# Encoder block on one core: window pooling moved from vector adds to banded matmuls, with the order of TensorE's work in that stage written out

## The chip, the cores and the metric

The kernel is one program on one core of a Trainium2 chip. Its time is the device time of one execution in microseconds (us); the number compared is the median over several executions. The engines are TensorE (PE, matmuls, with PEld for its weight loads), VectorE (DVE), ScalarE (ACT), GpSimd (POOL) and SyncE (SP), whose queue issues nearly all transfers.

## The reference, cut to what matters

An encoder block on 512 tokens of 1024 channels: a normalised input `h`, one wide projection of it, a pooling mixer and an eight-head differential attention side by side, then a mixture of 16 experts. The pooling mixer is what the change is about:

```python
h = rms_norm(x, g_mix[l])
z = jnp.einsum('bsd,dc->bsc', h, w_in[l])
u_pool = z[..., :c_q]                       # 1024 channels, 4 groups of 256
...
for g, w in enumerate((2, 4, 8, 16)):       # one window width for each group
    lo = jnp.clip(t - w // 2, 0, S)
    hi = jnp.clip(t + w // 2, 0, S)
    win = jnp.take(csg, hi, axis=1) - jnp.take(csg, lo, axis=1)
    cnt = (hi - lo).astype(jnp.float32)[None, :, None]
    pooled = (win / cnt).astype(u.dtype) - ug[:, :, g]
    outs.append(jnp.einsum('bsc,cd->bsd', pooled, w_mix[g]))
```

For each channel, the mean over a window of tokens, less the token itself, goes through a 256x256 matrix of its group.

## The kernel before

Operands of the early matmuls are kept as a high and a low part (`split`: ACT writes the rounded high part, then DVE or POOL the remainder), and each product is three matmuls (`mm3`: high-high, high-low, low-high). The stages in order are: the pooling stage; the projections for the first attention head (`scq`: q and k, then `task("v", 0)`); eight attention heads, with the other projections filled in between; the output projection; the router; 16 experts, whose weights are streamed into a ring of slots.

Weights of the early stages come through a queue of their own: `add_w` lists them, `load_next` issues the transfer on SP into one of four `wraw` buffers and splits it into one of three `whl` tiles, and `weights()` hands out the next tile and loads up to two ahead. A `whl` tile is refilled when the matmuls that read it are done. `CFG` says for each kind whether DVE (V) or POOL (G) makes the low part.

In the pooling stage the projection of a group (48 matmuls of 512 columns, the weights stationary and the 512 tokens moving) lands in the two PSUM banks of an `sc` tile, with channels on partitions and tokens along the free axis. `windows(g, sc)` then works on VectorE: it scales by the tokens' norm `rbc`, adds shifted copies in doubling steps until the window is full (one step for width 2, four for width 16), corrects 8 columns at either border, divides and subtracts, and splits the result into `pooled`. `mix(g)` multiplies that with the group's matrix (12 matmuls) into `ip` banks, and `mo` gets the split result. `ip` has two banks, `at` two, `sc` two pairs.

The order of instructions on each engine comes from a planner, which runs the program through a cost model. Its order on TensorE puts the matmuls of neighbouring steps between one another. Only the last expert has an order written out by hand (`tc.manual_schedule`).

Of the kernel before, what the change touches and what calls it, by code (L numbers as in the profile page):

```python
# [41 lines left out]
CFG = {'wu': 'GVGG',  # L42
# [20 lines left out]
 'fills': (1, 0.3, 2, 0.5, 2.5, 1.5, 2, 1, 0.5),  # L63
 'tabs': 1}
# [28 lines left out]
def block_kernel(tc, a, out):  # L93
# [105 lines left out]
    for g in GROUPS:  # L199
        for j in range(2):  # L200
            add_w(a["w_c"][2 * g + j], eng=ENG[CFG["wu"][GROUPS.index(g)]])
            if g != 3 and j == 1:
                add_w(a["w_pool_mix"][g + 1], 512, cfg("wmix"))
    add_w(a["w_c"][8], eng=cfg("wq0"))
    add_w(a["w_c"][16], eng=cfg("wk0"))
# [14 lines left out]
    for h in range(NH):  # L220
        for kind, i in plan(h):
            if kind == "q":
                add_w(a["w_c"][8 + i], eng=cfg("wq"))
            elif kind == "k":
                add_w(a["w_c"][16 + i], eng=cfg("wk"))
            elif kind == "v":
                add_w(a["w_v"][i, 0], eng=cfg("wv"))
                add_w(a["w_v"][i, 1], eng=cfg("wv"))
            elif kind == "pool":
                add_w(a["w_c"][24 + i], eng=cfg("wg"))  # L230
                add_w(a["w_pool_out"][i], eng=cfg("wp"))
            else:
                add_w(a["w_c"][32 + i], eng=cfg("wga"))
    for d in range(KT):
        add_w(a["w_attn_out"][d], eng=cfg("wao"))
        if d < 3:
            add_w(a["w_c"][37 + d], eng=cfg("wga"))
# [9 lines left out]
    with pool("st", side="right") as st:  # L247
        first = []
# [16 lines left out]
        def load_x(k):  # L265
            xk = st.tile([P, S], F32, name="xk", bufs=5)
# [4 lines left out]
        part_w(0, 0, P)  # L271
        load_x(0)
        part_w(0, P, S)
        part_w(1, 0, S)
        load_x(1)
        load_x(2)
        part_w(0, S, D)
        load_x(3)
        part_w(1, S, D)
        for k in range(4, KT):  # L280
            load_x(k)
        SP.dma_start(cv, a["consts"])
        load_next()
        sc0 = psA.tile([P, 2, S], F32, name="sc")
        for k in range(KT):
            for j in range(2):
                w = loaded[j]
                mm3(sc0[:, j], w[:, 0, cols(k)], w[:, 1, cols(k)], hT[:, 0, k], hT[:, 1, k], k == 0, k == KT - 1)
# [12 lines left out]
        pr = bank("at")  # L301
        for t in range(NTT):
            T.transpose(pr[:, cols(t)], rn[:, t:t + 1].to_broadcast([P, P]), ident)
        A.copy(rbc, pr)
# [3 lines left out]
        bd = pl.tile([P, 4, 2, PAD], F32, name="bd")  # L308
        SP.dma_start(bd, a["border"])
        SP.dma_start(psc, a["pool_scale"])  # L310
        V.tensor_scalar(psc, psc, 0.5, None, op0=ALU.mult)
        pooled = {}

        def windows(g, sc):
            w = WINDOWS[g]
            pooled[g] = pl.tile([P, 2, 2, S], F32R, name="pooled", bufs=2)
            n = S + 2 * PAD
            for j in range(2):
                u = pl.tile([P, n], F32, name="u", bufs=2)
                V.memset(u[:, 0:PAD], 0.0)  # L320
                V.memset(u[:, S + PAD:], 0.0)
                V.tensor_tensor(u[:, PAD:S + PAD], sc[:, j], rbc, op=ALU.mult)
                cur, lo, hi, d = u, 0, n, 0
                while (1 << d) < w:
                    nx = pl.tile([P, n], F32, name="sw", bufs=2)
                    if d == 0:
                        V.tensor_tensor(nx[:, 1:n], cur[:, 0:n - 1], cur[:, 1:n], op=ALU.add)
                        lo = 1
                    else:
                        q = 1 << (d - 1)  # L330
                        V.tensor_tensor(nx[:, lo + q:hi - q], cur[:, lo:hi - 2 * q], cur[:, lo + 2 * q:hi],
                                        op=ALU.add)
                        lo, hi = lo + q, hi - q
                    cur = nx
                    d += 1
                for b, o in ((0, PAD), (1, S)):
                    V.tensor_tensor(cur[:, o:o + PAD], cur[:, o:o + PAD], bd[:, g, b], op=ALU.mult)
                pq = pl.tile([P, S], F32, name="pq", bufs=2)
                V.scalar_tensor_tensor(pq, cur[:, PAD:S + PAD], 1.0 / w, u[:, PAD:S + PAD],
                                       op0=ALU.mult, op1=ALU.subtract)  # L340
                split(pooled[g][:, 0, j], pooled[g][:, 1, j], pq)
# [11 lines left out]
        def tables():  # L353
# [11 lines left out]
            pi, ang, nt, sh, ch = (st.tile([P, S], F32, name="xk", bufs=5) for _ in range(5))  # L365
# [19 lines left out]
        windows(3, sc0)  # L385
        for g in GROUPS[1:]:
            sc = psA.tile([P, 2, S], F32, name="sc")
            for j in range(2):
                run(hmul(sc[:, j], weights()))
            windows(g, sc)  # L390
            mix(g + 1)
            if g == CFG["tabs"]:
                tables()
        MASK = list(range(8, 16)) + list(range(8)) + list(range(16, 32))
        at_cm = pool("at", side="right")
        scq = psA.tile([P, 2, S], F32, name="sc")
        run(hmul(scq[:, 0], weights()))
        run(hmul(scq[:, 1], weights()))
        mix(0)
# [591 lines left out]
def _shape_constants():  # L991
# [11 lines left out]
    border = np.ones((4, 2, PAD), np.float32)  # L1003
    for g, w in enumerate(WINDOWS):
        cnt = np.clip(t + w // 2, 0, S) - np.clip(t - w // 2, 0, S)
        r = np.float32(w) / cnt.astype(np.float32)
# [89 lines left out]
```

## Time and profile before

| what | value |
|---|---|
| median of 3 runs | 1809.09 us (1806.86 to 1811.04) |
| the profiled execution | 1810.21 us, of which its span is 1808.4 us |
| TensorE busy (matmuls) | 1694.5 us, 94% of the span |
| VectorE, ScalarE, GpSimd busy | 570.6 us (32%), 339.3 us (19%), 220.0 us (12%) |
| bytes moved | 607.00 MB |
| mean granted TensorE clock | 0.973 |

Busy times are sums over the whole span, which has stages with different limits; a matmul's modelled duration overlaps the next one's, so the number of matmuls in a stretch says more than the busy time. The granted clock has no row before 11.8 us; the windows print 1.00 there.

### The profile page before, as it was taken

The page shows a single profiled execution, that of the slowest core. Times are in us where ns is not written, and L with a number is a line of the kernel's source. Part 1 is how long each engine was busy: PE and PEld are TensorE (multiplying, and loading weights), DVE is VectorE, ACT ScalarE, POOL GpSimd, SP SyncE. Part 2 cuts the span into 40 slices and gives each one's busy share as a digit, 9 for nine tenths or more (in the row PEclk, how much of TensorE's full clock was granted, in tenths as well). Part 3 has the DMA queues.
Part 4 walks back from the last instruction along what each step waited for, and adds up shares of the span by engine and source line. Part 5 has one row for each costly group of instructions (what it writes and reads, how often), then busy time and mean ns, then how long its engine had stood idle before and what let it go on. Part 6 is the DMA issues. An engine that isn't in the chain of part 4 may idle for free.

```text
span 1808.4 us, 20272 instructions
## 1 busy us (share of the span) xinstructions
PE 1694.5 (94%) x8296; PEld 863.2 (48%) x8296; DVE 570.6 (32%) x1330; ACT 339.3 (19%) x668; POOL 220.0 (12%) x193
## 2 busy tenths in 40 slices
PE   7999999999999999999999999998898989888898
PEld 5777887877873333333333333333333323233344
DVE  6865566663342212021220211122021212202023
ACT  4454555663221000000000000000000000000002
POOL 2453344444410000000000000000000000000000
PEclk9999999999999898998989999899999999999999
DMA  6332322222599999999999999999999999999997
GB/s 202 97 102 82 94 82 77 76 71 88 200 430 418 389 422 430 429 429 430 430 429 428 430 429 430 429 429 429 429 429 430 429 429 429 430 429 430 426 425 298
DMA packets 58973, 607.00 MB, mean 336 GB/s; under 512 B 8056, under 2 KB 8832, under 8 KB 32768
## 3 DMA queue, kind: packets, MB, share of 16 engines
q1 hardware_dynamic: 56320, 601.51, 80.0%
q0 software_dynamic: 2560, 4.20, 1.1%
q8 instruction: 65, 1.06, 0.2%
q14 instruction: 28, 0.23, 0.0%
HBM read 599.38 MB, written 2.10 MB: 333 GB/s over the span
## 4 chain that ended last, share of the span: by engine, by line
PE 53%; DMA 16%; DVE 7%; ACT 1%; issue 1%; POOL 0%; POOLq 0%; ACTq 0%; DVEq 0%
PE gu L786 23%; DMA sl<-in_w_down_dram 14%; PE mx L838 10%; PE mx L847 6%; PE mx L750 3%; DVE cmp L643 3%; DMA sl<-in_w_end_dram 2%; PE ip L124 1%; PE ip L125 1%; PE ip L123 1%; PE gu L885 1%; DVE cmp L646 1%; DVE ax L849 1%; PE gu L787 1%; PE gu L125 1%
## 5 line engine op out<-in xcount | busy, mean ns | idle before, releaser
L786 PE MATMUL gu<-sl,xs 128*64 128x512 f32 (+3 forms) x1556 | 626.7, 558 | 4.9 <-DMA sl<-in_w_up_dram 3.1
L787 PE MATMUL gu<-sl,xs 128*64 128x512 f32 (+3 forms) x1556 | 626.7, 558 | 0.0
L786 PEld LDWEIGHTS gu<-sl,xs 128*64 128x64 f32 x1556 | 209.4, 139 | 394.2 <-issue 377.4
L838 PE MATMUL mx<-sl,ax 128*64 128x512 f32 (+1 forms) x720 | 290.7, 559 | 34.7 <-DMA sl<-in_w_down_dram 29.0
L839 PE MATMUL mx<-sl,ax 128*64 128x512 f32 (+1 forms) x720 | 290.7, 559 | 0.0
L787 PEld LDWEIGHTS gu<-sl,xs 128*64 128x64 f32 x1556 | 209.4, 139 | 0.0
L838 PEld LDWEIGHTS mx<-sl,ax 128*64 128x64 f32 x720 | 95.8, 137 | 215.5 <-issue 158.7
L849 DVE TENSOR_TENSOR ax<-ax,mx 128x512 f32<-128x512 f32 x112 | 73.7, 685 | 384.9 <-PE mx L847 384.9
L118 POOL TENSOR_TENSOR whl<-wraw,whl 128x512 fp32r<-128x512 f32 x122 | 165.6, 1366 | 223.4 <-ACT whl L116 220.0
L960 POOL TENSOR_TENSOR fs<-fs,cv 128x1 f32<-128x1 f32 x4 | 2.6, 660 | 1269.0 <-DVE fs L959 1268.9
L792 DVE TENSOR_TENSOR act<-act,gu 128x512 f32<-128x512 f32 (+3 forms) x49 | 30.6, 629 | 393.3 <-PE gu L787 393.2
L847 PE MATMUL mx<-y,vv 64*128 64x512 f32 x240 | 118.6, 816 | 25.5 <-DVE ax L849 14.3
L116 ACT ACTIVATE whl<-wraw 128x512 fp32r<-128x512 f32 (+1 forms) x149 | 92.6, 625 | 102.1 <-PE ip L124 38.9
L643 DVE TENSOR_SCALAR_CACHE_REDUCE cmp<-mx,aff 128x384 f32<-128x384 f32 (+3 forms) x105 | 54.7, 521 | 148.9 <-PE mx L730 146.2
L123 PE MATMUL ip<-hT,whl 128*128 128x512 f32 x240 | 97.8, 407 | 0.0
L839 PEld LDWEIGHTS mx<-sl,ax 128*64 128x64 f32 x720 | 95.8, 137 | 0.0
L125 PE MATMUL ip<-hT,whl 128*128 128x512 f32 x240 | 94.5, 394 | 0.0
L124 PE MATMUL ip<-hT,whl 128*128 128x512 f32 x240 | 94.4, 393 | 0.0
L752 ACT COPY y<-mx 128x512 f32<-128x512 f32 x16 | 9.4, 585 | 452.8 <-PE mx L750 452.8
L847 PEld LDWEIGHTS mx<-y,vv 64*128 64x128 f32 x240 | 38.5, 222 | 100.4 <-DVE ax L849 76.1
L800 ACT COPY ax<-mx 128x512 f32<-128x512 f32 (+2 forms) x47 | 24.1, 549 | 310.6 <-PE mx L799 310.6
L750 PE MATMUL mx<-x,gm 128*64 128x512 f32 x256 | 58.4, 596 | 16.4 <-DVE gm L745 16.3
(246 smaller groups left out, 2007.6 us busy)
## 6 DMA issues: line engine op xcount, KB each, us to landing
sl<-in_w_gate_dram SPq DMA_DIRECT2D x60, 2816.0 KB, 33.3
sl<-in_w_up_dram SPq DMA_DIRECT2D x59, 2816.0 KB, 33.2
sl<-in_w_down_dram SPq DMA_DIRECT2D x56, 2816.0 KB, 31.2
wraw<-in_w_c_dram SPq DMA_DIRECT2D x79, 256.0 KB, 2.8
sl<-in_w_down_dram SPq DMA_DIRECT2D x8, 1408.0 KB, 12.2
sl<-in_w_end_dram SPq DMA_DIRECT2D x4, 2304.0 KB, 35.8
sl<-in_w_end_dram SPq DMA_DIRECT2D x6, 1280.0 KB, 25.6
sl<-in_w_end_dram SPq DMA_DIRECT2D x4, 1536.0 KB, 34.1
```

Source lines behind the costliest of these rows:

```text
L116: A.activation(dst_h, src, AF.Copy, scale=scale)
L118: (eng or V).tensor_tensor(dst_l, src, dst_h.bitcast(F32), op=ALU.subtract)
L123: T.matmul(ps, lh, rh, start=first, stop=False)
L124: T.matmul(ps, lh, rl, start=False, stop=False)
L125: T.matmul(ps, ll, rh, start=False, stop=last)
L643: V.tensor_scalar(scratch(src.shape[-1]), src, thr, None, op0=op, op1=ALU.add, accum_out=dst)
L750: T.matmul(px[cols(n, CAP)], gm[:, t], x1[:, t, cols(n, S)], start=(t == 0), stop=(t == NTT - 1))
L786: T.matmul(ps[0:CAP, :n], lhsT, r0, start=first, stop=last)
L787: T.matmul(ps[CAP:, :n], lhsT, r1, start=first, stop=last)
L838: T.matmul(pd[0:CAP, r], lhsT, w[:, o:o + n], start=first, stop=last)
L839: T.matmul(pd[CAP:, r], lhsT, w[:, o + n:o + 2 * n], start=first, stop=last)
L847: T.matmul(pc, vv[r, cols(t)], y[r], start=True, stop=True)
```

## The change

The projection of a pooling group is turned: tokens are on partitions (four tiles of 128) and the 256 channels of the group move, so the hidden state is stationary. It takes 96 matmuls of 256 columns instead of 48 of 512, with the weights laid out anew (`w_pu`). The token's norm is now applied when the projection is split out of PSUM (`evict`, with `rn` as a scale for each partition). The window is a banded 512x512 matrix, of which only blocks of 128 rows by 256 columns are used (`band`, made on the host and loaded by group): for each half of a group, eight matmuls of 256 columns and two of 8 columns give the pooled result in an `ip` bank. The adds on VectorE go, and so do `u`, `sw`, `pq` and the border factors. The first group's projection runs over the contraction outermost, and the first loads are cut so that weights and activations come in turn; all eight `xk` buffers exist. Three matmuls on a tile of zeros (512, 512 and 192 columns) stand ahead of everything. The pooling stage and the projections for q and k run on TensorE in the order in which `stage()` names them. The low part of the last group's weights moves from POOL to DVE ('GVGG' to 'GVGV'), and the list of weights is put in the new order.

```diff
-CFG = {'wu': 'GVGG',
+CFG = {'wu': 'GVGV',
...
     for g in GROUPS:
-        for j in range(2):
-            add_w(a["w_c"][2 * g + j], eng=ENG[CFG["wu"][GROUPS.index(g)]])
-            if g != 3 and j == 1:
-                add_w(a["w_pool_mix"][g + 1], 512, cfg("wmix"))
-    add_w(a["w_c"][8], eng=cfg("wq0"))
-    add_w(a["w_c"][16], eng=cfg("wk0"))
+        for half in range(2):
+            add_w(a["w_pu"][g, half], eng=ENG[CFG["wu"][GROUPS.index(g)]])
+        if g < 2:
+            add_w(a["w_pool_mix"][g + 2], 512, cfg("wmix"))
+    add_w(a["w_c"][0], eng=cfg("wq0"))
+    add_w(a["w_pool_mix"][1], 512, cfg("wmix"))
+    add_w(a["w_c"][8], eng=cfg("wk0"))
     add_w(a["w_pool_mix"][0], 512, cfg("wmix"))
...
+        zero = st.tile([P, S], F32, name="zero")
+        V.memset(zero, 0.0)
+        idle = bank("ip")
+        for n in (S, S, 192):
+            T.matmul(idle[:, :n], zero[:, :P], zero[:, :n], start=True, stop=True)
...
-            xk = st.tile([P, S], F32, name="xk", bufs=5)
+            xk = st.tile([P, S], F32, name="xk", bufs=KT)
             SP.dma_start(xk, a["xT"][k])
             split(hT[:, 0, k], hT[:, 1, k], xk, scale=gv[:, 0, k:k + 1])
 
         SP.dma_start(gv[:, 0], a["g_mix"])
-        part_w(0, 0, P)
-        load_x(0)
-        part_w(0, P, S)
-        part_w(1, 0, S)
-        load_x(1)
-        load_x(2)
-        part_w(0, S, D)
-        load_x(3)
-        part_w(1, S, D)
-        for k in range(4, KT):
-            load_x(k)
+        for c0, c1, ks in ((0, 256, (0,)), (256, 512, (1,)), (512, 1024, (2, 3))):
+            part_w(0, c0, c1)
+            for k in ks:
+                load_x(k)
+        for c0 in range(0, D, S):
+            part_w(1, c0, c0 + S)
+            for k in range(4 + c0 // 256, 6 + c0 // 256):
+                load_x(k)
         SP.dma_start(cv, a["consts"])
         load_next()
-        sc0 = psA.tile([P, 2, S], F32, name="sc")
+
+        def wide_step(u, t, ws, k):
+            w, c = ws[k // 4], cols(k % 4, 256)
+            mm3(u[t], hT[:, 0, k, cols(t)], hT[:, 1, k, cols(t)], w[:, 0, c], w[:, 1, c], k == 0, k == KT - 1)
+
+        sc = psA.tile([P, 2, S], F32, name="sc")
+        u3 = [sc[:, 0, :256], sc[:, 1, :256], bank("at")[:, :256], bank("at")[:, :256]]
         for k in range(KT):
-            for j in range(2):
-                w = loaded[j]
-                mm3(sc0[:, j], w[:, 0, cols(k)], w[:, 1, cols(k)], hT[:, 0, k], hT[:, 1, k], k == 0, k == KT - 1)
+            for t in range(NTT):
+                wide_step(u3, t, loaded[:2], k)
+        load_next()
         ss = st.tile([P, NTT], F32, name="ss")
         sst = st.tile([P, NTT], F32, name="sst")
...
-        pr = bank("at")
-        for t in range(NTT):
-            T.transpose(pr[:, cols(t)], rn[:, t:t + 1].to_broadcast([P, P]), ident)
-        A.copy(rbc, pr)
 
         pl_cm = pool("pl", side="right")
         pl = pl_cm.__enter__()
-        bd = pl.tile([P, 4, 2, PAD], F32, name="bd")
-        SP.dma_start(bd, a["border"])
         SP.dma_start(psc, a["pool_scale"])
         V.tensor_scalar(psc, psc, 0.5, None, op0=ALU.mult)
-        pooled = {}
-
-        def windows(g, sc):
-            w = WINDOWS[g]
+        band, ut, pooled = {}, {}, {}
+
+        def load_band(g):
+            raw = pl.tile([P, 3, 256], F32, name="braw", bufs=2)
+            SP.dma_start(raw, a["band"][g])
+            bh = pl.tile([P, 3, 256], F32R, name="bh", bufs=2)
+            bl = pl.tile([P, 2, PAD], F32R, name="bl", bufs=2)
+            A.activation(bh, raw, AF.Copy)
+            for i, (n, c) in enumerate(((0, slice(0, PAD)), (2, slice(256 - PAD, 256)))):
+                V.tensor_tensor(bl[:, i], raw[:, n, c], bh[:, n, c].bitcast(F32), op=ALU.subtract)
+            band[g] = bh, bl
+
+        def evict(g, u):
+            x = ut[g] = pl.tile([P, 2, NTT, 256], F32R, name="ut", bufs=2)
+            for t in range(NTT):
+                split(x[:, 0, t], x[:, 1, t], u[t], scale=rn[:, t:t + 1])
+
+        def product(g):
+            ws = (weights(1), weights(1))
+            sc = psA.tile([P, 2, S], F32, name="sc")
+            u = [sc[:, t // 2, cols(t % 2, 256)] for t in range(NTT)]
+            for t in range(NTT):
+                for k in range(KT):
+                    wide_step(u, t, ws, k)
+            evict(g, u)
+
+        def windows(g):
+            (bh, bl), x = band[g], ut[g]
             pooled[g] = pl.tile([P, 2, 2, S], F32R, name="pooled", bufs=2)
-            n = S + 2 * PAD
             for j in range(2):
-                u = pl.tile([P, n], F32, name="u", bufs=2)
-                V.memset(u[:, 0:PAD], 0.0)
-                V.memset(u[:, S + PAD:], 0.0)
-                V.tensor_tensor(u[:, PAD:S + PAD], sc[:, j], rbc, op=ALU.mult)
-                cur, lo, hi, d = u, 0, n, 0
-                while (1 << d) < w:
-                    nx = pl.tile([P, n], F32, name="sw", bufs=2)
-                    if d == 0:
-                        V.tensor_tensor(nx[:, 1:n], cur[:, 0:n - 1], cur[:, 1:n], op=ALU.add)
-                        lo = 1
-                    else:
-                        q = 1 << (d - 1)
-                        V.tensor_tensor(nx[:, lo + q:hi - q], cur[:, lo:hi - 2 * q], cur[:, lo + 2 * q:hi],
-                                        op=ALU.add)
-                        lo, hi = lo + q, hi - q
-                    cur = nx
-                    d += 1
-                for b, o in ((0, PAD), (1, S)):
-                    V.tensor_tensor(cur[:, o:o + PAD], cur[:, o:o + PAD], bd[:, g, b], op=ALU.mult)
-                pq = pl.tile([P, S], F32, name="pq", bufs=2)
-                V.scalar_tensor_tensor(pq, cur[:, PAD:S + PAD], 1.0 / w, u[:, PAD:S + PAD],
-                                       op0=ALU.mult, op1=ALU.subtract)
-                split(pooled[g][:, 0, j], pooled[g][:, 1, j], pq)
+                ps = bank("ip")
+                for t in (0, 3, 1, 2):
+                    uh, ul = x[:, 0, t, cols(j)], x[:, 1, t, cols(j)]
+                    n = (t + 1) // 2
+                    r = slice((0, 64, 192, 256)[t], (0, 64, 192, 256)[t] + 256)
+                    tc.keep_in_program_order(T.matmul(ps[:, r], uh, bh[:, n], start=t == 0, stop=False))
+                    if t in (0, 3):
+                        e = slice(0, PAD) if t == 0 else slice(S - PAD, S)
+                        T.matmul(ps[:, e], uh, bl[:, t // 3], start=False, stop=False)
+                    T.matmul(ps[:, r], ul, bh[:, n], start=False, stop=t == 2)
+                split(pooled[g][:, 0, j], pooled[g][:, 1, j], ps)
 
...
-        windows(3, sc0)
-        for g in GROUPS[1:]:
-            sc = psA.tile([P, 2, S], F32, name="sc")
-            for j in range(2):
-                run(hmul(sc[:, j], weights()))
-            windows(g, sc)
-            mix(g + 1)
-            if g == CFG["tabs"]:
-                tables()
+        def stage():
+            load_band(3)
+            evict(3, u3)
+            product(2)
+            pr = bank("ip")
+            for t in range(NTT):
+                T.transpose(pr[:, cols(t)], rn[:, t:t + 1].to_broadcast([P, P]), ident)
+            A.copy(rbc, pr)
+            load_band(2)
+            windows(3)
+            product(1)
+            mix(3)
+            tables()
+            load_band(1)
+            windows(2)
+            product(0)
+            mix(2)
+            load_band(0)
+            windows(1)
+            scq = psA.tile([P, 2, S], F32, name="sc")
+            run(hmul(scq[:, 0], weights()))
+            mix(1)
+            windows(0)
+            run(hmul(scq[:, 1], weights()))
+            mix(0)
+            return scq
+
         MASK = list(range(8, 16)) + list(range(8)) + list(range(16, 32))
         at_cm = pool("at", side="right")
-        scq = psA.tile([P, 2, S], F32, name="sc")
-        run(hmul(scq[:, 0], weights()))
-        run(hmul(scq[:, 1], weights()))
-        mix(0)
+        with tc.manual_schedule(engines={T.engine}):
+            scq = stage()
         pl_cm.__exit__(None, None, None)
...
-    border = np.ones((4, 2, PAD), np.float32)
+    band = np.zeros((4, P, 3, 256), np.float32)
     for g, w in enumerate(WINDOWS):
-        cnt = np.clip(t + w // 2, 0, S) - np.clip(t - w // 2, 0, S)
-        r = np.float32(w) / cnt.astype(np.float32)
-        border[g, 0], border[g, 1] = r[:PAD], r[S - PAD:]
-    border = np.broadcast_to(border, (P,) + border.shape).copy()
+        lo, hi = np.clip(t - w // 2, 0, S), np.clip(t + w // 2, 0, S)
+        full = ((t[:, None] >= lo) & (t[:, None] < hi)) * (np.float32(1) / (hi - lo).astype(np.float32)) - np.eye(S)
+        for n, (r, c) in enumerate(((0, 0), (P, 64), (3 * P, 256))):
+            band[g, :, n] = full[r:r + P, c:c + 256]
```

The places that read `w_c` count from the new start of that array, and `wide` is the layout that `w_v` already had.

## Rows read from the trace of the kernel before

**Rows 1.** Busy time by stretch: start:end, length, each engine's busy (count), clock, DMA share, GB/s.

```profile
5.30:11.80 6.50, 5.70 (x12) 3.63 (x13) 4.97 (x8) 4.81 (x8) 0.00 (x0) 1.00 0.96 332
11.80:20.20 8.40, 8.40 (x38) 6.90 (x37) 4.51 (x7) 5.40 (x9) 0.00 (x0) 1.00 0.98 337
20.20:38.20 18.00, 13.73 (x60) 10.37 (x58) 13.12 (x17) 7.80 (x15) 8.25 (x6) 1.00 0.58 184
38.20:42.50 4.30, 4.26 (x12) 3.21 (x13) 4.30 (x13) 0.25 (x1) 0.00 (x0) 0.61 0.09 26
...
53.40:59.50 6.10, 4.50 (x13) 3.21 (x13) 6.02 (x14) 3.07 (x6) 1.50 (x2) 0.73 0.27 87
59.50:86.20 26.70, 26.70 (x117) 21.65 (x115) 22.25 (x41) 12.78 (x20) 13.19 (x9) 1.00 0.27 83
...
98.40:480.00 381.60, 378.11 (x1957) 306.24 (x1957) 222.79 (x377) 195.27 (x389) 164.34 (x142) 1.00 0.28 85
480.00:1808.40 1328.40, 1230.54 (x5955) 488.08 (x5953) 271.93 (x816) 97.19 (x202) 17.51 (x18) 0.97 0.99 422
```

**Rows 2.** Waits of TensorE, 0 to 86.5 us: total us, times, longest.

```profile
...
PE ip L123 <- ACT pooled L116: 4.5, 2, 3.3
PE sc L125 <- DVE whl L118: 1.0, 1, 1.0
PE sc L123 <- ACT whl L116: 0.8, 1, 0.8
PE ip L124 <- DVE pooled L118: 0.4, 1, 0.4
```

**Rows 3.** Waits of SP's transfer queue, 480 to 500 us.

```profile
SPq L810 <- PE mx L125: 10.1, 1, 10.1
```

**Rows 4.** Groups of VectorE and ScalarE instructions, 0 to 100 us: count, busy us, mean ns.

```profile
L339 DVE SCALAR_TENSOR_TENSOR pq<-sw,u 128x512 f32<-128x512 f32 x8 | 7.7, 957 | 0.0
...
L120 DVE SCALAR_TENSOR_TENSOR vt<-ip,rn,vt 128x256 fp32r<-128x256 f32 x4 | 1.9, 480 | 1.4 <-ACT vt L116 1.4
L116 ACT ACTIVATE vt<-ip,rn 128x256 fp32r<-128x256 f32 x4 | 1.9, 469 | 3.4 <-PE ip L125 3.4
```

**Rows 5.** TensorE by stretch, while `task("v", ...)` runs matmuls of 256 columns.

```profile
86.52:95.05 8.53, 8.53 (x72) 1.00 0.35 107
...
183.20:187.30 4.10, 4.10 (x38) 1.00 0.33 122
```

**Rows 6.** Timeline, all engines, first loads: start, duration, engine, line, operation.

```profile
4.56 0.72 ACT L116 ACTIVATE hT<-xk,gv 128x512 fp32r<-128x512 f32 x1 [1.08 <-DMA xk<-in_xT_dram]
...
5.33 0.79 PE L123 MATMUL sc<-hT,whl 128*128 128x512 f32 x1 [5.33 <-ACT hT L116]
...
11.41 2.71 ACT L116 ACTIVATE hT<-xk,gv 128x512 fp32r<-128x512 f32 x4
...
23.65 1.04 POOL L113 TENSOR_TENSOR rn<-sst,cv 128x4 f32<-128x4 f32 x1 [22.34 <-DVE sst L112]
```

**Rows 7.** Timeline of TensorE: four transposes; 16 small matmuls; four of type f32.

```profile
24.74 0.65 PE L303 MATMUL at<-ident,rn 128*128 128x128 f32 x4
...
529.48 1.90 PE L671 MATMUL gu<-wr,act 128*128 128x16 f32 x16
531.23 1.54 PE L653 MATMUL gu<-x,ident 128*128 128x384 f32 x4
```

**Rows 8.** Timeline, all engines, from `mix(0)` to the first matmul of `task("v", 0)`.

```profile
84.57 0.39 PE L125 MATMUL ip<-pooled,whl 128*128 128x512 f32 x1
...
85.00 0.69 ACT L116 ACTIVATE mo<-ip,psc 128x512 fp32r<-128x512 f32 x1
...
85.72 0.75 DVE L120 SCALAR_TENSOR_TENSOR mo<-ip,psc,mo 128x512 fp32r<-128x512 f32 x1 [2.13 <-ACT mo L116]
...
85.96 0.40 PE L125 MATMUL ip<-pooled,whl 128*128 128x512 f32 x1
...
86.52 0.39 PE L123 MATMUL ip<-whl,hT 128*128 128x256 f32 x1 [0.16 <-DVE mo L120]
```

More of the change, by code (lines that the diff above doesn't have):

```diff
@@ L62 @@
  'pool': (2, 2, 2, 1, 1, 0, 0, 0),
- 'fills': (1, 0.3, 2, 0.5, 2.5, 1.5, 2, 1, 0.5),
- 'tabs': 1}
+ 'fills': (1, 0.3, 2, 0.5, 2.5, 1.5, 2, 1, 0.5)}
 NS1, NS2 = 4, 3
@@ L222, in block_kernel @@
             if kind == "q":
-                add_w(a["w_c"][8 + i], eng=cfg("wq"))
+                add_w(a["w_c"][i], eng=cfg("wq"))
             elif kind == "k":
-                add_w(a["w_c"][16 + i], eng=cfg("wk"))
+                add_w(a["w_c"][8 + i], eng=cfg("wk"))
             elif kind == "v":
@@ L229, in block_kernel @@
             elif kind == "pool":
[L230 removed]
+                add_w(a["w_c"][16 + i], eng=cfg("wg"))
                 add_w(a["w_pool_out"][i], eng=cfg("wp"))
             else:
[L233 removed]
+                add_w(a["w_c"][24 + i], eng=cfg("wga"))
     for d in range(KT):
@@ L236, in block_kernel @@
         if d < 3:
-            add_w(a["w_c"][37 + d], eng=cfg("wga"))
+            add_w(a["w_c"][29 + d], eng=cfg("wga"))
     for k in range(KT):
@@ L364, in tables @@
             le = st.tile([P, 2], F32, name="le")
-            pi, ang, nt, sh, ch = (st.tile([P, S], F32, name="xk", bufs=5) for _ in range(5))
+            pi, ang, nt, sh, ch = (st.tile([P, S], F32, name="xk", bufs=KT) for _ in range(5))
             pi = pi.bitcast(I32)
@@ L1002, in _shape_constants @@
     t = np.arange(S)
-    border = np.ones((4, 2, PAD), np.float32)
+    band = np.zeros((4, P, 3, 256), np.float32)
     for g, w in enumerate(WINDOWS):
-        cnt = np.clip(t + w // 2, 0, S) - np.clip(t - w // 2, 0, S)
-        r = np.float32(w) / cnt.astype(np.float32)
-        border[g, 0], border[g, 1] = r[:PAD], r[S - PAD:]
-    border = np.broadcast_to(border, (P,) + border.shape).copy()
+        lo, hi = np.clip(t - w // 2, 0, S), np.clip(t + w // 2, 0, S)
+        full = ((t[:, None] >= lo) & (t[:, None] < hi)) * (np.float32(1) / (hi - lo).astype(np.float32)) - np.eye(S)
+        for n, (r, c) in enumerate(((0, 0), (P, 64), (3 * P, 256))):
+            band[g, :, n] = full[r:r + P, c:c + 256]
     tie = (p[None, :] < p[:, None]).astype(np.float32)
     slots = np.broadcast_to(np.concatenate([np.arange(CAP)] * 2).astype(np.float32), (P, 2 * CAP)).copy()
-    return {"consts": cv, "border": border, "tie": tie, "slots": slots}
+    return {"consts": cv, "band": band, "tie": tie, "slots": slots}
 def down_blocks(w):
@@ L1043, in stat, with wide @@
         return w.reshape(KT, P, n, P).transpose(2, 1, 0, 3).reshape(n, P, D)
+    def wide(w):
+        return w.reshape(2, 4, P, 4, 256).transpose(3, 0, 2, 1, 4).reshape(4, 2, P, D)
     def pk(v):
@@ L1056, in _layout @@
         "g_mix": pk(i["g_mix"]),
-        "w_c": stat(np.concatenate([w_in[:, :3 * D], w_in[:, 4 * D:]], axis=1)),
-        "w_v": w_in[:, 3 * D:4 * D].reshape(2, 4, P, 4, 256).transpose(3, 0, 2, 1, 4).reshape(4, 2, P, D),
+        "w_c": stat(np.concatenate([w_in[:, D:3 * D], w_in[:, 4 * D:]], axis=1)),
+        "w_pu": wide(w_in[:, :D]),
+        "w_v": wide(w_in[:, 3 * D:4 * D]),
         "w_pool_mix": i["w_pool_mix"].reshape(4, 2, P, 256).transpose(0, 2, 1, 3).reshape(4, P, 512),
```

## The prediction

> **What bounds the kernel now.** I read the busy time by stretch first, since shares over the whole span mix stages. From 480 us on, the DMA engines are 99% busy at 422 GB/s: the expert weights set the pace there. From 98.4 to 480 us TensorE is busy in 378.1 of 381.6 us. [rows 1] What ties the two together is in the waits of SP's queue: the first expert transfers stand behind a matmul of the output projection (L125), the longest wait being 10.1 us. [rows 3] So whatever the front of the kernel saves on TensorE starts the stream earlier by as much, and nothing behind it can hide a gain or a loss of a few us. The question is when the last matmul of `mix(0)` ends: 85.96 us plus its 0.23, so 86.2 us. [rows 8]
>
> From the first matmul at 5.33 us [rows 6] to 86.2 us are 80.9 us. In the undisturbed stretch 59.5 to 86.2 us, 117 matmuls of 512 columns take 26.7 us, 0.228 us each. [rows 1] The stage has 288 of these (4x48 projections, 48 for q and k, 4x12 in `mix`), 65.7 us, and four transposes, some 0.4 us (0.65 with their tail) [rows 7]: 66.1 us. The other 14.8 us are lost. The waits after the start come to 0.8 + 1.0 + 4.5 + 0.4 = 6.7 us, of which 4.9 are for `pooled`, that is, for VectorE's window adds. [rows 2] A further 6.1 us is the low clock: the 12 matmuls from 5.3 to 11.8 us should take 2.7 us and take 5.7 without the wait of 0.8 (3.0 lost); 12 from 38.2 to 42.5 us, after the longest wait, lose 1.6 at a granted clock of 0.61; 13 from 53.4 to 59.5 us, after the other waits, lose 1.5 at 0.73. [rows 1] Some 2 us are left over, in dearer matmuls of `mix` and records that are missing.
>
> **The change, part by part.** *VectorE's adds go.* Eight `pq` alone take 7.7 us [rows 4], and the adds, scalings and border factors with them. The new `evict` is 16 pairs at 0.47 (ACT) and 0.48 us (DVE) [rows 4], 7.5 and 7.7 us in 80 us; VectorE, 13.1 of 18 us busy where TensorE waited longest, and full from 38.2 to 42.5 us [rows 1], has room. What this buys is only the 4.9 us of waits and the two low-clock spells behind them (3.1 us): 8.0 us.
>
> *Projections of 256 columns.* `task("v", 0)` has the same form: 72 in 8.53 us with a tail, 0.118 each; later, 36 that start in 4.10 us (two of the row began before it), 0.114. [rows 5] I take 0.115: 96 x 0.115 = 11.0 us a group, as dear as 48 x 0.228 = 10.9. The bounds over the stage's 448 matmuls of this width are -0.5 and +1.3 us. The Trainium skill (TensorE: Matmul & The Clock Gate, Back-to-back issue gap) gives 262 cycles for 256 columns, 0.109 us at 2.4 GHz; by that figure the sum would be 2.7 us lower, but the rows have the measured spacing and decide.
>
> *The band matmuls.* For each group two halves of eight matmuls of 256 columns and two of 8. The small ones have no row; the nearest are 16 of 16 columns that start 0.109 us apart (529.48 to 531.23). [rows 7] Below, they could cost nearly nothing behind a weight load, above, as much as a wide one. So 8 x (8 x 0.115 + 2 x 0.11) = 9.1 us, between 7.4 and 9.4. This is new work on the engine that sets the end.
>
> *The first product.* Its first matmul waits for the first `hT` part: 4.56 us, when its data lands, plus 0.72, to 5.33. [rows 6] The weight piece ahead of it is twice as long, so I put it at 5.45 us. Each step of the contraction is 12 matmuls, 1.4 us at the high clock. The eighth `hT` part was made at about 14.1 us (11.41 + 2.71) [rows 6], when five `xk` buffers held the loads back; so the feed ends no later and, if TensorE keeps 1.4 us a step from 5.45 on, the last step begins at 15.3: the feed hides. What is open is the clock. After the wait that ended at 38.24 us it was high again by 42.5; at the start, with a wait of 0.8 us in between, not before 11.8. [rows 1, 2] The three zero matmuls have 1216 columns of type f32; four of 384 take 1.54 us with their tail at the high clock [rows 7], so 1.2 us, or 2.4 at half of it: from about 1.4 us they end before 4 us and delay nothing. Whether they count as work for the clock no row shows. I take the high clock at 9.7 us, 4.3 us after the first matmul, as from 38.24 to 42.5, without any help of the zeros: at half the clock a matmul of 256 columns takes 2 x 256 / 2.4 GHz = 0.213 us, so 20 of them, then 76 at 0.115, to 18.4 us. Bounds: 16.5 (high from the start) and 19.5 us (high at 11.8).
>
> *The order written out.* Then come three products, 3 x 11.04 = 33.1 us; bands, 9.1; `mix`, 48 x 0.23 = 11.0; q and k, 48 x 0.228 = 10.9; transposes, 0.4. That is 64.5 us, to 82.9. Nothing can now be put into a gap, so each wait counts in full. The norm `rn` was ready at 24.7 us [rows 6]; one more weight tile is asked for ahead of `x`, about 1.5 us more of transfer, and four evictions of 0.5 us make 28.5 us, against the first band matmul at 18.4 + 11.0 + 0.4 = 29.8: hidden by 1.3 us. Each `whl` tile is free one product or more before it is wanted. But thrice a `windows` stands right behind a `mix`, and takes the two `ip` banks that `mix` has just filled. Rows 8 show this handover in front of `task("v", 0)`: last matmul of the first bank at 84.57, ACT to 85.69, DVE to 86.47, next matmul at 86.52, though TensorE was free at 86.19: 0.33 us late. [rows 8] The second bank follows 1.4 us later, of which the first half's 1.15 us of band matmuls cover all but 0.25. Thrice 0.58 is 1.7 us if ACT and DVE answer at once. Below, nothing; above, an instruction of 0.7 us ahead of either on its queue, for both banks: 3 x 2 us.
>
> *Also.* The SP queue gets four `band` loads of 0.4 MB and one less small load; after 20 us the DMA engines are at most 58% busy [rows 1], so they hide. Behind ACT's `bh` copy stand the evictions; at 768 elements it takes under 1 us, within the 1.3 above. The last group's low parts move from POOL to a VectorE that has been relieved: nothing.
>
> The sum: 82.9 + 1.7 = 84.6 us against 86.2, so -1.6 us. The profiled execution took 1810.21 us, 1.1 above the median, and becomes 1808.6; the median of 1809.09 becomes **1807.5 us**.
>
> **The rivals.**
> 1. *Gain as hoped.* The zeros bring the high clock before 5.45 us (16.5 instead of 18.4: -1.9), the handovers hide behind other banks' work (-1.7), and matmuls are at 0.114 (-0.5): with the -1.6 above, -5.7 us, 1803.4. Faster by the bound of 0.2% (3.6 us, about what a measurement of this kernel can tell from no change) from half of these three on. For it: nothing in rows 2 waits but for VectorE and the first loads. Against: no row shows zeros at work, and rows 8 show the handover. The Trainium skill (same page, Part 1) says that the throttled clock is the default and activity releases it; no run here shows whether zeros do.
> 2. *Late clock.* If it rises at 11.8 us as before, the first product ends at 19.5, 1.1 us later: -0.5 us, 1808.6. No change.
> 3. *The handover becomes the new bound.* ACT and DVE take their instructions in the planner's order; a weight split that waits for a `whl` tile, ahead of `mo` on ACT, holds both `ip` banks, and TensorE with its fixed order stands. At the bound of 2 us each, three handovers cost 6.0 instead of 1.7, and one low-clock spell as after 53.4 us adds 1.5: +4.2 us, 1813.3. It decides (+3.6 us) once the three cost over 5.4 us, 1.8 us each, with the clock falling once. For it: that very spell followed waits of 1.2 and 0.4 us in all. [rows 1, 2] Against: in the six stretches of rows 1 up to 86.2 us ACT is busy in 34.1 of 70.0 us. [rows 1]
> 4. *The shift is lost.* The planner orders the attention stage anew and eats it: 1809.1. Against: that stage has 3.5 us of idle in 381.6 [rows 1]; there is little room either way.
>
> **How the numbers follow.** My forecast (between -3.6 and +1 us) gets 0.31, the late clock 0.10, the lost shift 0.07: 0.48 for no change. Rival 1 and parts of it beyond -3.6 us: 0.36. Rival 3 beyond +3.6: 0.16. The likeliest one's own range is 1805.5 to 1810.1. The range that leaves out about 2 in 10 reaches from just past rival 1, 1803.0, to just short of rival 3, 1812.0.
>
> **What would show it.** In the new profile: band matmuls near 0.115 us and the 8-column ones near 0.11; first product ending near 18.4 us, and the granted clock rising once, before 10 us, and staying; waits of TensorE for `mo` and `pooled` of 0.3 us each behind `mix`, in place of 4.9 us for `pooled`; `task("v", 0)` starting near 84.9 instead of 86.52 us, and everything behind it shifted alike. The prediction is wrong if a wait of over 2 us stands in the stage (rival 3), if `task("v", 0)` starts before 83 us (rival 1), or if the attention stage changes its length by over 1 us.

## The result and the profile after

The changed kernel takes 1821.66 us (median of 5 runs, 1815.88 to 1822.03) beside 1809.42 for the kernel before in the same comparison: ratio 1.0057, 95% interval 1.0042 to 1.0073. Forecast were 1807.5 us, in a range from 1803.0 to 1812.0. By the ratio it is slower by some 10 us, and the prediction was wrong in sign and range. Its profiled execution took 1817.18 us, with a span of 1815.4.

Where the time went is read best from one row, the start of `task("v", 0)`, the first matmul behind the changed stage. Here is TensorE's timeline of the changed kernel at four places: the start, the end of `mix(3)`, the start of the last `windows`, and the start of that task.

```profile
1.46 3.85 PE L252 MATMUL ip<-zero 128*128 128x512 f32 x6 [1.46 <-DVE zero L249]
5.47 0.38 PE L122 MATMUL sc<-whl,hT 128*128 128x256 f32 x1 [0.17 <-ACT hT L115]
5.70 0.28 PE L123 MATMUL sc<-whl,hT 128*128 128x256 f32 x1
5.81 0.29 PE L122 MATMUL at<-whl,hT 128*128 128x256 f32 x1
...
47.80 0.40 PE L124 MATMUL ip<-pooled,whl 128*128 128x512 f32 x1
52.23 0.47 PE L349 MATMUL ip<-bh,ut 128*128 128x256 f32 x1 [4.03 <-DVE mo L119]
...
83.93 0.39 PE L349 MATMUL ip<-bh,ut 128*128 128x256 f32 x1 [2.08 <-DVE mo L119]
...
86.39 0.40 PE L122 MATMUL sc<-hT,whl 128*128 128x512 f32 x1
...
95.02 0.39 PE L122 MATMUL ip<-whl,hT 128*128 128x256 f32 x1 [0.17 <-DVE mo L119]
```

The task starts at 95.02 us where it started at 86.52 [rows 8]: 8.5 us late, not 1.6 early. The waits of TensorE up to there, which answer to [rows 2]:

```profile
PE ip L349 <- DVE mo L119: 6.3, 3, 4.0
PE ip L252 <- DVE zero L249: 1.5, 1, 1.5
PE ip L349 <- ACT rbc L405: 1.3, 1, 1.3
PE sc L122 <- ACT hT L115: 0.8, 2, 0.6
PE sc L124 <- DVE hT L119: 0.5, 2, 0.3
```

The waits for `pooled` and for weights are gone. In their place the first band matmul (L349) of three `windows` waits for `mo`, the eviction of the `mix` in front of it, 4.03, 0.17 and 2.08 us, and one more waits 1.3 us for `rbc`, the copy that empties the `ip` bank of the transposes. (The 1.5 us for `zero` lie ahead of the first matmul.) The busy time by stretch, with the columns of [rows 1], shows what the longest wait did:

```profile
5.47:18.73 13.26, 12.14 (x97) 11.41 (x97) 10.32 (x16) 9.48 (x15) 0.00 (x0) 1.00 0.94 325
18.73:29.60 10.87, 10.87 (x98) 10.87 (x97) 2.62 (x9) 7.55 (x15) 1.09 (x2) 1.00 0.74 277
...
33.93:45.23 11.30, 11.30 (x98) 11.30 (x97) 5.68 (x14) 4.03 (x9) 1.88 (x2) 1.00 0.61 190
...
48.20:52.23 4.03, 0.00 (x1) 0.01 (x1) 4.03 (x9) 4.00 (x9) 0.64 (x1) 1.00 0.57 192
52.23:56.23 4.00, 4.00 (x21) 4.00 (x22) 3.62 (x7) 1.44 (x3) 0.63 (x1) 0.57 0.45 138
```

While TensorE stands from 48.20 to 52.23 us, VectorE and ScalarE are busy in all of it (the first and second pair after PEld). Behind the wait `windows(2)` takes 4.00 us at a granted clock of 0.57; `windows(0)`, at the high clock, takes 2.46 (83.93 to 86.39), so the spell costs 1.5 us more.

Which instructions those were is in ScalarE's timeline of the changed kernel:

```profile
36.86 0.47 ACT L115 ACTIVATE ut<-sc,rn 128x256 fp32r<-128x256 f32 x1 [0.90 <-DVE ut L119]
41.63 0.20 ACT L390 ACTIVATE le<-ls 128x2 f32<-128x2 f32 x1 [4.30 <-DVE ls L376]
43.89 0.85 ACT L321 ACTIVATE bh<-braw 128x768 fp32r<-128x768 f32 x1 [2.05 <-DMA braw<-in_band_dram]
44.76 1.28 ACT L387 ACT_TABLE_LOAD   x1
46.27 0.63 ACT L387 ACTIVATE xk<-xk 128x512 f32<-128x512 f32 x1 [0.22 <-DVE xk L386]
46.80 1.14 ACT L115 ACTIVATE whl<-wraw 128x512 fp32r<-128x512 f32 x2
47.84 0.71 ACT L389 ACTIVATE xk<-xk,cv 128x512 f32<-128x512 f32 x1
48.46 0.61 ACT L115 ACTIVATE whl<-wraw 128x512 fp32r<-128x512 f32 x1
48.98 0.45 ACT L115 ACTIVATE ut<-sc,rn 128x256 fp32r<-128x256 f32 x1
49.34 0.62 ACT L115 ACTIVATE whl<-wraw 128x512 fp32r<-128x512 f32 x1
49.85 0.67 ACT L115 ACTIVATE mo<-ip,psc 128x512 fp32r<-128x512 f32 x1
...
51.92 0.68 ACT L115 ACTIVATE mo<-ip,psc 128x512 fp32r<-128x512 f32 x1
...
81.89 0.63 ACT L115 ACTIVATE whl<-wraw 128x512 fp32r<-128x512 f32 x1 [3.65 <-PE ip L124]
82.42 0.67 ACT L115 ACTIVATE mo<-ip,psc 128x512 fp32r<-128x512 f32 x1
```

ScalarE first stands idle for 4.30 us at the Exp of the tables (`le`), whose data comes from VectorE, which waits for the `lam` vectors; then 2.05 us for `braw`; then it loads the Sin table and waits for VectorE again. Weight splits and the `ut` of the next group pile up behind, and when `mix(3)` has filled its first bank, at about 46.6 us (six matmuls of 0.23 us before its end at 48.03), six instructions stand between the Sin and the first `mo`. VectorE's part of it follows at 51.43 us, behind a split and an eviction of its own. The Trainium skill (Perfetto Trace Analysis, Tensor Engine Instruction) says that ScalarE's and VectorE's execution queues are strictly first in, first out; the trace agrees: `mo`, whose bank was full at 46.6 us, starts behind all six, at 49.85. At 81.89 it is one weight split that waits 3.65 us, for a matmul of `mix(1)`, and `mo` comes after it.

Behind the stage little differs. From the start of `task("v", 0)` to the first gather matmul (535.76 us before, 545.85 after) the two executions take 449.2 and 450.8 us; the difference is one more low-clock spell near 322 us. The expert stage took 1272.6 us before and 1269.5 after. So 8.5 + 1.6 - 3.1 = 7.0, the difference of the two profiled executions. The expert stage changes by a few us from execution to execution; the 10.1 us at its start match the ratio (0.0057 x 1809.4 = 10.3). The queue that ties the stages together shows as before [rows 3]:

```profile
SPq L839 <- PE mx L124: 9.5, 1, 9.5
```

### The profile page after: what moved, and what is told of

Its sections match the earlier page's. It is cut to its first block, busy times and chain, and to the rows that moved or that the text cites. A ratio compares the mean times of both kernels' runs of the same rounds, so it can differ in the third digit from the quotient of the medians.

```text
span 1815.4 us, 20811 instructions
## 1 busy us (share of the span) xinstructions
PE 1706.0 (94%) x8574; PEld 882.6 (49%) x8574; DVE 546.8 (30%) x1291; ACT 348.3 (19%) x688; POOL 210.1 (12%) x189
## 4 chain that ended last, share of the span: by engine, by line
PE 52%; DMA 15%; DVE 7%; ACT 1%; issue 1%; POOL 0%; POOLq 0%; ACTq 0%; DVEq 0%
PE gu L815 23%; DMA sl<-in_w_down_dram 14%; PE mx L867 10%; PE mx L876 6%; PE mx L779 3%; DVE cmp L672 3%; DMA sl<-in_w_end_dram 2%; PE ip L123 1%; PE ip L124 1%; PE ip L122 1%; DVE cmp L675 1%; DVE ax L878 1%; PE gu L914 1%; PE gu L816 1%; PE gu L124 1%
## 5 line engine op out<-in xcount | busy, mean ns | idle before, releaser
L117 POOL TENSOR_TENSOR whl<-wraw,whl 128x512 fp32r<-128x512 f32 x118 | 155.7, 1328 | 241.1 <-ACT whl L115 222.4
```

The costliest lines, as they stand in the source:

```text
L117: (eng or V).tensor_tensor(dst_l, src, dst_h.bitcast(F32), op=ALU.subtract)
```

## The experiments

The theory from this profile (A): `windows` takes the two `ip` banks that `mix` has just filled, and their evictions stand behind other work on ScalarE and VectorE; with the order written out, TensorE has nothing else to do. Rivals: the fixed order itself is the cost (B); the tables' late transfers alone are; or there is a new cost in the band matmuls, the 256-column matmuls or the zeros (C). Medians of the kernel before stand with each run.

**The changed kernel once more**, no edit.

> The changed kernel once more, beside the experiments on the same chip. All theories: 1.004 to 1.007 of the kernel before, with the same three waits behind mix (4.0, 0.2 and 2.1 us) and task v starting near 95 us.

1819.27 us, ratio 1.0058 (1.0038 to 1.0077); waits for `mo` 6.7 us, the longest 4.5; task v at 96.64 us, gather at 545.83. It repeats.

**The window sums in the other bank.**

```diff
-                ps = bank("ip")
+                ps = bank("at")
                 for t in (0, 3, 1, 2):
```

> Only the bank changes: the band matmuls write to the 'at' banks, idle in this stage, instead of the 'ip' banks that mix has just filled. Theory A (the loss is the handover of the ip banks, held by evictions that stand late in ScalarE's queue): the waits for mo behind mix (6.3 us), the wait for rbc (1.3) and the low-clock spell behind the longest (1.6) go, task v starts at 85 to 86 us instead of 95.0, and the time falls by 8 to 10 us to 0.999 to 1.001 of the kernel before. Rival B (the fixed order itself: TensorE stands wherever any operand is late): the waits come back under other names, task v starts at 91 us or later. Rival C (the added matmul work is the loss, the waits cover nothing else): under 2 us gained.

1806.99 us (before: 1809.99), ratio 0.9991 (0.9981 to 1.0002): one word takes away the whole loss, some 12 us. TensorE's waits from 0 to 95 us, the evictions of `mix(3)` on ScalarE and the start of task v in this run:

```profile
PE ip L252 <- DVE zero L249: 1.5, 1, 1.5
PE ip L122 <- DVE vt L119: 0.5, 1, 0.5
PE sc L124 <- DVE hT L119: 0.3, 1, 0.3
PE ip L122 <- DVE mo L119: 0.2, 1, 0.2
```

```profile
48.88 0.67 ACT L115 ACTIVATE mo<-ip,psc 128x512 fp32r<-128x512 f32 x1
...
51.25 0.68 ACT L115 ACTIVATE mo<-ip,psc 128x512 fp32r<-128x512 f32 x1
```

```profile
83.75 0.39 PE L122 MATMUL ip<-whl,hT 128*128 128x256 f32 x1 [0.17 <-DVE mo L119]
```

The evictions are about as late as before (48.88 and 51.25 beside 49.85 and 51.92, though the first bank is full 2.1 us earlier, at 44.5), with the same Sin, Exp and splits ahead of them, yet nobody waits. So lateness alone costs nothing; lateness together with the shared bank does. This is A, and it rules out a new cost in the matmuls: all band matmuls and zeros are still there. The Trainium skill (Perfetto Trace Analysis, Matmuls) asks that independent matmul groups rotate through different PSUM banks, so that the eviction of one overlaps the matmuls of the next; the two runs agree, 6.3 us of waits for `mo` against 0.2.

**The tables' transfers issued earlier**, ahead of `product(2)`; the arithmetic stays.

```diff
         def stage():
             load_band(3)
             evict(3, u3)
+            pi = tables_load()
             product(2)
...
-            tables()
+            tables(pi)
```

> Only the transfers of the tables (lambda vectors, positions, g_subln) are asked for earlier, ahead of the second product; banks and TensorE's order in the stage stay. Theory A in its narrower form (ScalarE stood from 37 to 46 us on table instructions whose transfers were late, with the evictions behind them): the wait of 4.0 us and its low-clock spell go, the one of 2.1 us stays, task v starts near 89 us, 5 to 6 us less than the changed kernel. If what holds ScalarE is the planner's order as such, the 4.0 us stay. Rival C: no change.

1816.53 us (before: 1809.99), ratio 1.0044 (1.0027 to 1.0061), task v at 93.17 us, not 89. The first long wait fell from 4.03 to 0.31 us, as it should if the late transfers hold it. But the tables' arithmetic now keeps VectorE busy from 28.4 to 32.8 us; ScalarE's next `ut` waits for VectorE, and a weight split of `product(1)` stands behind it:

```profile
33.26 0.47 ACT L115 ACTIVATE ut<-sc,rn 128x256 fp32r<-128x256 f32 x1 [2.13 <-DVE ut L119]
...
35.83 0.63 ACT L115 ACTIVATE whl<-wraw 128x512 fp32r<-128x512 f32 x1
```

TensorE waits 2.5 us for that split and 1.0 for one on POOL. Much of the gain was given back there: the backlog moved to another place.

**The stage's order left to the planner.**

```diff
-        with tc.manual_schedule(engines={T.engine}):
-            scq = stage()
+        scq = stage()
```

> Only the written-out order goes: the planner orders TensorE in the stage. Rival B (the fixed order is the loss): the waits shrink since other matmuls are put between, task v starts by 88 us, 6 us or more gained. Theory A: the planner does not foresee the late evictions, so the longest wait stays in part and less than 4 us are gained. Rival C: no change.

1813.91 us (before: 1809.99), ratio 1.0029 (1.0016 to 1.0041), task v at 93.19 us; a wait of 2.6 us for `mo` at 52.48 stays. The gain of 5.4 us lies between the two expectations. So B explains at most half: the planner can put other work into some of the gap, but with the bank shared a loss remains.

**Both parts of `mo` on VectorE.**

```diff
-                split(mt[:, 0], mt[:, 1], ps, scale=psc[:, 2 * g + c:2 * g + c + 1])
+                s = psc[:, 2 * g + c:2 * g + c + 1]
+                V.tensor_scalar(mt[:, 0], ps, s, None, op0=ALU.mult)
+                V.scalar_tensor_tensor(mt[:, 1], ps, s, mt[:, 0].bitcast(F32), op0=ALU.mult, op1=ALU.subtract)
```

> The changed kernel with both parts of the evictions of mix (mo) on VectorE; ScalarE no longer takes part in them, and the banks stay shared. Theory: what held the two ip banks was ScalarE's queue (the Sin and Exp of the tables and the weight splits ahead of mo), so the second long wait (2.08 us, behind a weight split) falls under 0.7 us, and the first (4.03 us) to between 0.5 and 2.5 us, since VectorE also works on the tables; task v starts at 90 to 92.5 us, the time is 1813 to 1817 us. Rival: VectorE was as late as ScalarE: both waits stay, 1819 us.

1816.61 us (before: 1809.38), ratio 1.0046 (1.0028 to 1.0063), task v at 94.30 us. Two rows of TensorE:

```profile
52.13 0.58 PE L349 MATMUL ip<-bh,ut 128*128 128x256 f32 x1 [4.99 <-DVE mo L366]
...
82.89 0.39 PE L349 MATMUL ip<-bh,ut 128*128 128x256 f32 x1 [0.23 <-DVE mo L366]
```

The last wait falls from 2.08 to 0.23 us, as expected: that one was ScalarE's weight split. The first grows to 4.99, a miss, and task v with it: VectorE is as deep in the tables and splits at that time as ScalarE.

**The tables called later**, behind `mix(1)`; and the same with `mo` on VectorE.

```diff
             mix(3)
-            tables()
...
             mix(1)
+            tables()
```

> The changed kernel with the tables moved, transfers and all, from behind mix(3) to behind mix(1); the banks stay shared. Theory: what stands ahead of mo in the queues of ScalarE and VectorE sets each wait, so the first long wait (4.03 us at 48.03) falls under 0.8 us without new waits for weights, while the one ahead of the last windows (2.08 us) stays or grows, because the tables are now near it; task v starts at 89 to 92.5 us, the time is 1813 to 1817 us. Rival: the tables were not the holder and the first wait stays above 2 us, or it only turns into waits for weights as when the transfers were moved early: 1816 to 1820 us.

> Both: the tables behind mix(1), and both parts of mix's evictions on VectorE; the banks stay shared. Theory: with the tables away from the first handover and the weight splits away from the last one, the waits for mo sum to under 2 us and task v starts at 86 to 89 us, 1808.5 to 1812 us; what is left against separate banks (83.75 us, 1806.99 us) is the wait for rbc and the ends of the evictions themselves. Rival: the handover is slow for another reason (semaphores, the two evictions in series on one engine): the waits stay above 4 us and the time above 1815 us.

1818.25 us (before: 1809.86), ratio 1.0058 (1.0040 to 1.0076), and 1819.06, ratio 1.0057 (1.0039 to 1.0076). First waits of 4.6 and 6.0 us: both missed. In both traces Exp and Sin run between 43.5 and 52 us, beside 41.6 to 48.6 in the changed kernel: only TensorE's order is fixed, and the planner put the other engines' work close to where it had been, still around the first handover. The edit did not move the tables behind `mix(1)`, so these runs say nothing on what their absence there is worth. (The last wait did fall to 0.23 us again in the second of them.)

**The tables left out**; and the same with `mo` on VectorE.

```diff
         def tables():
             SP.dma_start(gs, a["g_subln"])
             V.tensor_scalar(gs, gs, (1.0 - LAM_INIT) * 0.5, None, op0=ALU.mult)
-            lv = st.tile([P, 4, HD], F32, name="lv")
...
-            V.tensor_tensor(Ct, sh, rbc, op=ALU.mult)
+            V.memset(nlam, -0.5)
+            V.memset(St, 0.0)
+            V.memset(Ct, 1.0)
```

> The changed kernel with the work of the tables left out: their five transfers, the chain on VectorE, Sin and Exp are gone, and Ct, St and nlam are constants, so attention's numbers are not the reference's. The banks stay shared. (Moving the call had moved nothing: the planner put the same operations at the same time, 43 to 53 us, so that run did not test the theory.) Theory: the backlog that the tables' chain leaves on ScalarE and VectorE is what holds mo at the first long wait; without it that wait falls from 4.03 us to under 0.8 us and the low-clock spell behind it goes, while the second (2.08 us, a weight split ahead of mo) and rbc's (1.27 us) stay; task v starts at 89 to 91 us, the time is 1813 to 1816 us. Rival: the weight splits and the evictions of the product alone are enough; the first wait stays over 2 us and the time over 1817 us.

> The tables left out in the same way, and both parts of mix's evictions on VectorE. Theory: both holders are gone, so the waits for mo sum to under 2 us with no change to the banks; rbc's wait stays; task v starts at 86 to 88.5 us, the time is 1809 to 1812 us. Rival: sharing the banks costs by itself, whatever the queues hold: waits for mo stay above 3 us, task v above 90 us.

1811.16 us (before: 1809.23), ratio 1.0014 (1.0002 to 1.0027), and 1814.74, ratio 1.0029 (1.0017 to 1.0041). TensorE in the first of them:

```profile
47.39 0.39 PE L349 MATMUL ip<-bh,ut 128*128 128x256 f32 x1 [0.30 <-DVE mo L119]
...
78.14 0.39 PE L349 MATMUL ip<-bh,ut 128*128 128x256 f32 x1 [2.22 <-DVE mo L119]
90.78 0.39 PE L122 MATMUL ip<-whl,hT 128*128 128x256 f32 x1 [0.17 <-DVE mo L119]
```

Without the tables the first wait is 0.30 instead of 4.03 us, the second stays at 2.22, and task v starts at 90.78, within the 89 to 91 expected (the time is 2 us under its range). So the tables' chain held the first handover and a weight split the last. With `mo` on VectorE too the last wait falls to 0.23 us, but two evictions one behind the other on one engine make five smaller waits, 2.6 us in all; task v starts at 89.12, outside the 86 to 88.5 expected. Emptying the queues gives back 5.9 of the 11.3 us that a bank of its own gives at task v (95.02, 89.12 and 83.75 us). The medians of the two runs do not follow their traces: the second is 3.6 us longer, outside its 1809 to 1812 us, though both its task v and its gather (538.88 beside 541.99 us) come earlier. The runs do not show why, so only the start of task v is read from them.

**The zeros' share.** The version with separate banks without the zeros, and the kernel before with the zeros alone.

```diff
-        zero = st.tile([P, S], F32, name="zero")
-        V.memset(zero, 0.0)
-        idle = bank("ip")
-        for n in (S, S, 192):
-            T.matmul(idle[:, :n], zero[:, :P], zero[:, :n], start=True, stop=True)
```

> The changed kernel with the window sums in bank at (the earlier run with that edit alone: 1806.99 us, task v starting at 83.75 us) and without the zero matmuls. Theory: the zeros hold the clock high for the first product. Without them its first matmuls run at 0.22 instead of 0.113 us until the clock rises; the first product ends at 20.5 to 21.5 us instead of about 18.7, task v starts at 86 to 86.5 us, the time is 1809 to 1810 us, that of the kernel before. Rival: the first product waits for hT's tiles anyway, so a slow start costs under 0.5 us: 1807 us.

> The kernel before with the zero tile and the three zero matmuls alone; the pooling stays as it was. Theory: the zeros are a part with a worth of its own: the first product's low-clock start goes (the first matmul ends its 0.44 us spacing for 0.22 us), task v starts 2 to 3 us earlier than 86.52 us, and the time is 1806.5 to 1808 us. Rival: the loads set the end of the first products, and the time stays at 1809.5 to 1810.5 us.

With separate banks and no zeros: 1808.19 us (before: 1809.38), ratio 0.9995 (0.9984 to 1.0005). Its first product:

```profile
11.62 0.40 PE L124 MATMUL sc<-whl,hT 128*128 128x256 f32 x1
11.83 0.31 PE L122 MATMUL sc<-whl,hT 128*128 128x256 f32 x1
11.98 0.28 PE L123 MATMUL sc<-whl,hT 128*128 128x256 f32 x1
12.10 0.28 PE L124 MATMUL sc<-whl,hT 128*128 128x256 f32 x1
```

Matmuls start 0.21 us apart up to 11.83 us and 0.11 to 0.12 after it. With the zeros they do so at most up to 7.4 us. In the changed kernel's trace they are 0.11 to 0.12 apart from the first row on (5.70, 5.81), but in the one with separate banks, the one to compare with, the change comes here:

```profile
7.17 0.42 PE L122 MATMUL sc<-whl,hT 128*128 128x256 f32 x1
7.39 0.33 PE L123 MATMUL sc<-whl,hT 128*128 128x256 f32 x1
7.56 0.28 PE L124 MATMUL sc<-whl,hT 128*128 128x256 f32 x1
```

The first product then ends at 19.7 instead of 18.2 us (expected: 20.5 to 21.5), and task v starts at 86.89 instead of 83.75 us (expected: 86 to 86.5). Of these 3.1 us, the first product accounts for 1.5. Most of the rest are two waits for weight splits ahead of `product(0)`, 0.43 and 0.49 us with the restarts behind them, that the other trace does not have; whether the zeros spare them, no run shows. The medians, 1808.19 and 1806.99 us, do not separate the two versions.

In the kernel before the zeros gain nothing: 1811.47 us (expected: 1806.5 to 1808), ratio 1.0016 (1.0005 to 1.0027), task v at 87.22 instead of 86.52. TensorE and ScalarE ahead of task v say why:

```profile
83.72 0.40 PE L125 MATMUL ip<-pooled,whl 128*128 128x512 f32 x1
87.22 0.38 PE L123 MATMUL ip<-whl,hT 128*128 128x256 f32 x1 [3.10 <-DVE mo L120]
```

```profile
84.66 1.15 ACT L116 ACTIVATE whl<-wraw 128x512 fp32r<-128x512 f32 x2 [4.53 <-DMA wraw<-in_w_c_dram]
85.71 0.67 ACT L116 ACTIVATE mo<-ip,psc 128x512 fp32r<-128x512 f32 x1
```

The last matmul of `mix(0)` ends at 83.95 us, 2.2 us earlier than in [rows 8]. Then the `ip` bank is held, since `mo` stands on ScalarE behind two weight splits that wait for a transfer, and TensorE stands for 3.10 us. So the gain goes in the very handover that costs 0.33 us in [rows 8]: the shared bank has this price in the kernel before, too.

**Separate banks and the planner's order.** The version that comes out of these: bank `at` for the window sums, and no `manual_schedule`.

> The changed kernel with the window sums in bank at and TensorE's order of the stage left to the planner. Theory (the shared bank is the whole cost, the fixed order none): waits for mo and rbc stay away, task v starts at 83.5 to 84.5 us, 1806 to 1808 us. Rival (the fixed order has a worth or a price of its own once the banks are apart): task v starts more than 1.5 us from 83.75 us, and the time goes with it by as much.

1806.83 us (before: 1809.38), ratio 0.9984 (0.9973 to 0.9994), task v at 83.11 us and gather at 532.34. It is the only version here whose interval lies wholly on the faster side of the kernel before, by about 3 us. Once the banks are apart, fixing the order is worth nothing (83.75 and 83.11 us).

## Why the prediction was wrong

The step that failed is the handover: "Thrice 0.58 is 1.7 us if ACT and DVE answer at once", with the upper bound "an instruction of 0.7 us ahead of either on its queue, for both banks: 3 x 2 us". They did not answer at once. The three waits for `mo` sum to 6.3 us; `rbc`, which the prediction never counted among the holders of an `ip` bank, adds 1.3; the low-clock spell adds 1.5. That is 9.1 us instead of 1.7. Rival 3 named the mechanism, the bank held behind a weight split in the planner's order, and for the last handover it came to the letter; but its price of 2 us a handover was drawn from one instruction ahead of the eviction on either queue, where six stood on ScalarE, and [rows 8] show a handover at which both queues happened to be nearly empty (with the zeros in the kernel before, the same one cost 3.10 us). The first handover cost twice the bound. And the argument against it, ScalarE busy in 34.1 of 70.0 us, is an average: from 48.20 to 52.23 us it was busy in 4.00 of 4.03.

The other terms, against 84.6 us for the end of `mix(0)` and 94.7 measured:

- The first product ended at 18.7 us, forecast 18.4, but for two wrong reasons that cancel. The zeros did raise the clock (forecast: not before 9.7 us), and the feed did not hide: 1.3 us of waits for `hT` (0.17 ahead of the first matmul), and the restarts behind them.
- The zeros themselves were mis-sized, though in this trace they delayed nothing: forecast 1.2 or 2.4 us, ending before 4 us; they took 3.85, to 5.31 us. The row of four in [rows 7] was misread: a matmul of type f32 leaves two rows (three of them leave six here), so that row is two matmuls of 384 columns, and the 16 small ones are eight.
- Three products: 10.9 + 11.3 + 11.3 = 33.5 us, forecast 33.1. The price of a 256-column matmul was right (0.113 to 0.118 us).
- Four `windows` at 2.46 us: 9.8, forecast 9.1. A matmul of 8 columns cost the 0.11 us that were forecast: the next one starts 0.03 us after it, and the one behind that 0.20 later instead of 0.12. `mix`, q and k: 0.3 us above the forecast in sum.
- Together: 0.3 + 0.4 + 0.7 + 0.3 + (9.1 - 1.7) = 9.1 of the 10.1 us. The last 1.0 us is, by the rows, 0.17 us ahead of each of the four waits (a row ends 0.17 us after the next matmul could start: 48.20 and 48.03 us) and 0.3 us in `windows(1)`, which is late for its second bank.

Right were also that `rn` and the evictions of `product` hide (no wait for `ut`), that the relief of VectorE takes the waits for `pooled` away, and that a shift at the stage's end reaches the end of the kernel: 8.5 us at task v are 10.1 at the gather, and with separate banks 2.8 us earlier gave 1.1 there in that execution and 3.4 earlier gave 3.4 in the last version. With separate banks, where no handover is left, `mix(0)` ends at 83.4 us; the sum without handovers gave 82.9. So apart from the handovers the sum was right to within 0.5 us, by luck in its first product. The last sign of being wrong came true as well, 450.8 us for the attention stage beside 449.2, but by a low-clock spell; over all the runs here this stretch takes 447.8 to 453.0 us.

That the two queues hold the banks is shown (the bank changed, the tables left out, `mo` moved). Why the planner put Exp and Sin just there is argued from the late `lam` and `braw` rows alone.

## What to carry to other kernels

When an order is written out for one engine, price each place where a step takes a buffer that the step before it has just filled, by the longest queue that the evicting engine can have there, not by a handover where it was idle; then look whether another bank is free at that moment, which costs one word. A gain ahead of such a handover can be lost in it: the zeros bring the end of `mix(0)` 2.2 us forward in the kernel before, and task v starts no earlier. And moving a call in the program hardly moved its work on the engines whose order the planner sets.

## What the runs showed of the hardware

- Matmuls on zeros count for the clock. In the twelve traces with six rows of them from 1.46 us on, the spacing of the first product's matmuls shows the high level of 2.4 GHz by 7.4 us at the latest, in seven of them from the first or second one on; in the two traces without them it shows 1.2 GHz until 11.7 and 11.8 us. The Trainium skill (TensorE: Matmul & The Clock Gate, Part 1) says that the default is throttled and activity releases it; these traces agree, and show that matmuls on zeros release it too.
- In the version without zeros the granted-clock column reads 1.00 from 5.76 to 11.80 us as well, where the matmuls ran at half speed: at the start of a span the level is to be read from the spacing of the matmuls, not from the column.
- An almost identical wait need not have the same effect: 2.0 us for `aT` stand in the attention stage of both profiled executions, and the clock fell after it in the changed kernel's alone (3.60 us at 0.53, 1.6 us lost). The wait of 2.08 us ahead of `windows(0)` did not lower it either.
